# First up products cut by columns, GpSimd's sums behind the last norm, and the final residual in two bulk transfers

## The chip, the cores and the metric

The kernel runs on one core of a Trainium2 chip. The metric is the device time of one execution in microseconds (us), and the runs of a kernel are summed up by their median. The engines of the core work side by side, each through its own list of instructions in order, and wait for each other by semaphores: TensorE (PE; its weight loads are listed as PEld), VectorE (DVE), ScalarE (ACT), GpSimd (POOL), and SyncE (SP), which here issues nearly all transfers.

## The reference

One layer of a diffusion backbone on 128 context tokens and 512 latent tokens (640 in all), width 1024, in fp32. A mixer (pooling and neighbourhood attention, merged and projected) comes first, then the channel part, in which nearly all of the change lies:

```
def _conv_ffn(h, w_up, conv_w, conv_b, w_down):
    u = h @ w_up
    up = jnp.pad(u, ((0, 0), (1, 1), (0, 0)))
    u = up[:, :-2] * conv_w[0] + up[:, 1:-1] * conv_w[1] + up[:, 2:] * conv_w[2] + conv_b
    a, g = jnp.split(u, 2, axis=-1)
    return (jax.nn.silu(a) * g) @ w_down
...
    x = x + ga * _merge(pool, na, gp, gn, w_pool_proj, w_na_proj, w_o)
    h = _modulated_norm(x, norm_ffn_g, sf, cf)
    x = x + gf * _conv_ffn(h, w_up, ffn_conv_w, ffn_conv_b, w_down)
```

w_up is 1024 x 5632 (halves a and g of 2816 columns), w_down 2816 x 1024. The outputs are the two new x and the context's keys and values.

## The kernel before, in words

**Arithmetic.** A product of fp32 matrices is made of three matmuls: both factors are split into a high part (ScalarE rounds it, names ending in h or hi) and a low part (VectorE subtracts the high one from the original, names ending in l or lo; `split_to`, L132), and high x high, high x low and low x high are added up.

**Tokens.** There are five token tiles of 128; tile 0 is the context. The channel part works on two halves of the columns of the transposed h: the first half has HB = 322 columns (tiles 0 and 1 and the first 64 columns of tile 2, with margins for the convolution), the second half 320. `b1h`/`b1l` hold the first half of all eight blocks of 128 features, `b12h`/`b12l` and `b2h`/`b2l` the second half of features 0 to 511 and 512 to 1023.

**The end of the mixer.** The output product (L736 to L738) runs tile by tile; `residual` adds x, the norm of the tile is taken (L743 to L747, result `xn`), and `second_h` (L753) transposes the tile on TensorE (L759), scales and shifts it (L764, L767) and splits it into b1, b12 and b2. Its call for tile 4 stands after the first up products.

**The up product.** Its 22 groups f of 128 columns of a and of g are computed as follows. Group 0 goes plainly: `plain` (L899) multiplies 16 weight blocks with the first half of the columns, 48 matmuls, and later with the second half. From group 1 on, seven products take the place of eight, after Strassen's scheme: `up_a(f)` makes the two that need only original weights (A11 B11, A12 B21), while GpSimd makes four sums of weight blocks (`ws`, L859 to L862) from the raw loads; `up_w(f)` splits these sums and a22; `products_b` makes the other five with sums of h (`th`, `tl`; VectorE, L791 to L794 and L799). The last of the five, with A22, may start when VectorE has read the accumulator that it adds to (L888). `conv` makes the convolution for a and g: one step on ScalarE (L923), two on VectorE (L924, L925); then SiLU and the product (L941: GpSimd, for the last group VectorE), and the split into `ahi`/`alo`, for the last group into `th`/`tl`.

**The down product.** Every second f, `down_group` multiplies two groups with their rows of w_down (weights `dhi`/`dlo`, raw loads `raw<-in_wdn`), in ten pieces of a token tile and 512 columns, and VectorE adds each to `acc` (L978). The last four groups are done in `down_last` (L980): the first four pieces are begun early in accumulators of their own, up to their last group; each finished piece is added to acc (L1001), multiplied by the gate gf (`gfb`, L1002), and the residual x is added (L1003), which was stored in DRAM (`xscr`) and comes back piece by piece through `xr` (L999, three buffers). The last piece is cut in two of 256 columns.

**What sets the order.** The code is written in program order, and a scheduler sets the order of each engine from its own timeline; `keep_in_program_order` and `issue_after` pin single instructions. A pool with n buffers makes a writer wait until the reader of n earlier is done: `raw` has three, `ws` one. SP issues loads in its order, so one that waits for its buffer holds up those behind it.

## Time and profile before

| | us |
|---|---|
| median of three runs | 909.35 |
| lowest, highest | 908.69, 910.04 |
| the profiled execution | 908.53 |
| its span (first to last event in the trace) | 906.7 |
| TensorE busy in the span | 869.7 |
| VectorE busy | 669.9 |
| ScalarE busy | 394.6 |
| GpSimd busy | 232.9 |

Starts are counted from the start of the span. A row of a timeline gives start, duration, engine, line and operation, what it writes and reads, and in brackets how long its engine stood idle before and what ended that wait. Matmuls are pipelined: the time from start to start is what one costs, not its duration. The granted clock (PEclk) is that of TensorE, 1.00 for 2.4 GHz and 0.50 for 1.2 GHz.

### The profile page before, as it was taken

What the parts mean: (1) busy time and instruction counts of PE and PEld (TensorE: products, weight loads), DVE (VectorE), ACT (ScalarE), POOL (GpSimd) and SP (SyncE); (2) the same over time, 40 slices, a digit from 0 to 9 for tenths busy, and PEclk for the clock granted to TensorE, in tenths of its full rate; (3) what the DMA queues carried; (4) which work ended last, traced back from release to release, by engine and by line L of the source; (5) the groups of instructions that cost most, each with busy time, mean ns of one, the idle gap of its engine ahead of it and who ended that gap; (6) DMA issues with size and microseconds to landing.
All of it is one profiled execution on the core that took longest, in us unless ns stands there. A gap on an engine that the chain in (4) does not pass through costs nothing.

```text
span 906.7 us, 13346 instructions
## 1 busy us (share of the span) xinstructions
PE 869.7 (96%) x5234; PEld 781.0 (86%) x5234; DVE 669.9 (74%) x1000; ACT 394.6 (44%) x710; POOL 232.9 (26%) x179
## 2 busy tenths in 40 slices
...
DMA packets 33023, 112.20 MB, mean 124 GB/s; under 512 B 3856, under 2 KB 4528, under 8 KB 32704
## 3 DMA queue, kind: packets, MB, share of 16 engines
...
q14 instruction: 22, 0.18, 0.1%
...
## 4 chain that ended last, share of the span: by engine, by line
PE 77%; DVE 9%; DMA 7%; ACT 3%; issue 2%; POOL 1%; SPq 0%; DVEq 0%; ACTq 0%; POOLq 0%
PE acc L837 23%; PE acc L219 21%; PE sm L964 4%; PE sm L966 4%; PE sm L965 4%; PE acc L203 3%; PE acc L205 3%; PE acc L204 3%; DVE wlo L134 2%; ACT whi L133 2%; DMA raw<-in_wo 2%; DMA na<-in_xl 2%; DVE cv L924 1%; DMA raw<-in_wdn 1%; PE sm L541 1%
## 5 line engine op out<-in xcount | busy, mean ns | idle before, releaser
L133 ACT CAST whi<-raw 128x1024 fp32r<-128x1024 f32 (+1 forms) x86 | 81.2, 945 | 193.6 <-PE acc L837 77.0
L134 DVE TENSOR_TENSOR wlo<-raw,whi 128x1024 fp32r<-128x1024 f32 (+1 forms) x86 | 102.7, 1195 | 39.7 <-ACT whi L133 39.1
L837 PE MATMUL acc<-th,whi 128*128 128x322 f32 (+1 forms) x336 | 103.8, 313 | 4.2 <-ACT whi L133 2.2
L837 PE MATMUL acc<-tl,whi 128*128 128x322 f32 (+1 forms) x336 | 104.5, 311 | 0.0
L837 PE MATMUL acc<-th,wlo 128*128 128x322 f32 (+1 forms) x336 | 104.0, 311 | 0.0
L219 PE MATMUL acc<-hhi,whi 128*128 128x320 f32 x320 | 92.3, 322 | 0.4 <-ACT t L440 0.4
L219 PE MATMUL acc<-hlo,whi 128*128 128x320 f32 x320 | 90.1, 315 | 0.0
L219 PE MATMUL acc<-hhi,wlo 128*128 128x320 f32 x320 | 89.3, 315 | 0.0
L859 POOL TENSOR_TENSOR ws<-raw 128x512 f32<-128x512 f32 x21 | 30.7, 1462 | 176.5 <-DVE wlo L134 105.1
L965 PE MATMUL sm<-dlo,ahi 128*128 128x512 f32 (+1 forms) x188 | 74.0, 393 | 0.0
L964 PE MATMUL sm<-dhi,ahi 128*128 128x512 f32 (+1 forms) x188 | 71.4, 395 | 2.2 <-ACT dhi L133 1.7
L966 PE MATMUL sm<-dhi,alo 128*128 128x512 f32 (+1 forms) x188 | 71.4, 394 | 0.0
L837 PEld LDWEIGHTS acc<-th,whi 128*128 128x128 f32 x336 | 63.1, 189 | 8.0 <-ACT whi L133 4.4
L837 PEld LDWEIGHTS acc<-tl,whi 128*128 128x128 f32 x336 | 63.4, 189 | 1.4
L837 PEld LDWEIGHTS acc<-th,wlo 128*128 128x128 f32 x336 | 63.3, 189 | 1.2
L133 ACT CAST whi<-ws 128x1024 fp32r<-128x1024 f32 x42 | 43.1, 1047 | 42.6 <-PE acc L837 40.6
L219 PEld LDWEIGHTS acc<-hhi,whi 128*128 128x128 f32 x320 | 58.9, 193 | 2.8 <-issue 1.5
L837 PE MATMUL acc<-b1l,whi 128*128 128x322 f32 x184 | 57.6, 315 | 3.8 <-DVE b1l L134 3.8
L978 DVE TENSOR_TENSOR acc<-sm,acc 128x512 f32<-128x512 f32 x80 | 53.1, 682 | 9.2 <-PE sm L966 9.2
L219 PEld LDWEIGHTS acc<-hlo,whi 128*128 128x128 f32 x320 | 58.8, 192 | 0.8 <-issue 0.7
L219 PEld LDWEIGHTS acc<-hhi,wlo 128*128 128x128 f32 x320 | 58.2, 191 | 0.7 <-issue 0.5
L837 PE MATMUL acc<-b1h,whi 128*128 128x322 f32 x184 | 57.2, 314 | 0.9 <-ACT b1h L133 0.9
...
## 6 DMA issues: line engine op xcount, KB each, us to landing
...
```

Of the source, the lines that this page charges most:

```text
L133: nc.scalar.copy(hi, raw)
L134: nc.vector.tensor_tensor(out=lo, in0=raw, in1=hi.bitcast(F32), op=SUB)
L203: nc.tensor.matmul(ps[t], lhsT=xh, rhs=wh, start=(kt == 0), stop=False)
L204: nc.tensor.matmul(ps[t], lhsT=xh, rhs=wl, start=False, stop=False)
L205: nc.tensor.matmul(ps[t], lhsT=xl, rhs=wh, start=False, stop=(kt == KT - 1))
L219: nc.tensor.matmul(o[:, :n], lhsT=w[:, k], rhs=cut(x, k, c, n), start=st and a, stop=sp and b)
L837: upped[0] = nc.tensor.matmul(ps[:, cs], lhsT=a[:, c], rhs=b[:, k, cs], start=start and first, stop=last, skip_group_check=skip and not st ...
L859: nc.gpsimd.tensor_tensor(out=s[:, 1], in0=a21, in1=a22, op=ADD)
L964: nc.tensor.matmul(ps, lhsT=xh, rhs=hi[:, sl], start=first and j == js[0], stop=False)
L965: nc.tensor.matmul(ps, lhsT=xh, rhs=lo[:, sl], start=False, stop=False)
L966: nc.tensor.matmul(ps, lhsT=xl, rhs=hi[:, sl], start=False, stop=last and j == js[-1])
L978: nc.vector.tensor_tensor(out=o, in0=ps, in1=o, op=ADD)
```

## The change

Four edits. (1) `pool_mix`, the pooling mixer, is issued behind the last matmul of the gate products (`issue_after`). (2) `plain` makes its products in two cuts of the columns, 0 to 258 for both a and g, then 258 to 322; the ends of the first cut are the columns of tiles 0 and 1. (3) Of the four sums of group 1 on GpSimd, the third is written second, and the first and third wait for the norm of tile 4; the a22 split of group 1 stays in program order. (4) In `down_last` the stored x comes back in two transfers of 128 x 2560 elements into b1l and b1h, which nobody reads by then. For pieces 4 to 10, GpSimd multiplies acc by the gate and adds x ahead of the product, piece 4 behind the split of the last group; VectorE then multiplies the product by the gate into `tmp` and adds it.

```diff
@@ -131,7 +131,7 @@
 
     def split_to(raw, hi, lo):
         nc.scalar.copy(hi, raw)
-        nc.vector.tensor_tensor(out=lo, in0=raw, in1=hi.bitcast(F32), op=SUB)
+        return nc.vector.tensor_tensor(out=lo, in0=raw, in1=hi.bitcast(F32), op=SUB)
 
     def load_w(src, own=None):
         r = load_raw(src)
@@ -207,6 +207,8 @@
     def halves(w, kk):
         return tuple(x[:, kk * 512:(kk + 1) * 512] for x in w)
 
+    mt_last = [None]
+
     def mt_steps(outs, whi, wlo, xhi, xlo, nk, ncol, cut=lambda x, k, c, n: x[:, k, c:c + n]):
 
 
@@ -216,7 +218,8 @@
             st, sp = k == 0, k == nk - 1
             for w, x, a, b in ((wh, xhi, True, False), (wh, xlo, False, False), (wl, xhi, False, True)):
                 for o, (c, n) in zip(outs, ncol):
-                    nc.tensor.matmul(o[:, :n], lhsT=w[:, k], rhs=cut(x, k, c, n), start=st and a, stop=sp and b)
+                    i = nc.tensor.matmul(o[:, :n], lhsT=w[:, k], rhs=cut(x, k, c, n), start=st and a, stop=sp and b)
+                    mt_last[0] = i.ins
             yield
 
     def run(steps):
@@ -637,10 +640,12 @@
             split_to(pw, pwh, pwl)
         split_to(na[:, g, :], nhi[:, g, :], nlo[:, g, :])
         if pend:
-            pool_mix(*pend)
+            with tc.issue_after(mt_last[0]):
+                pool_mix(*pend)
         pend = (g, *d)
     t2s[4] = gate_na(4)
-    pool_mix(*pend)
+    with tc.issue_after(mt_last[0]):
+        pool_mix(*pend)
     eg.close()
     en.close()
     ex = ExitStack()
@@ -727,6 +732,8 @@
     for t in range(5):
         residual(acc[t], t, 0, sq0)
 
+    normed = []
+
     def out_product(t, mid):
         ps = ps_acc()
         for kt in range(KT):
@@ -744,7 +751,7 @@
         nc.scalar.activation(std, std, AF.Sqrt, bias=eps, scale=1.0 / D)
         nc.vector.reciprocal(std, std)
         xn = fp.tile([P, D], F32, name="xn2", bufs=2)
-        nc.scalar.activation(xn, x1[:, t, :], AF.Copy, scale=std)
+        normed.append(nc.scalar.activation(xn, x1[:, t, :], AF.Copy, scale=std).ins)
         return xn
 
 
@@ -856,9 +863,15 @@
         nc.scalar.copy(p1, pa[:, :HB])
         nc.vector.tensor_tensor(out=us["a"][f % 2][:, 1:1 + HB], in0=pb[:, :HB], in1=p1, op=ADD)
         s = fw.tile([P, 4, 512], F32, name="ws", bufs=1)
-        nc.gpsimd.tensor_tensor(out=s[:, 1], in0=a21, in1=a22, op=ADD)
+        first = nc.gpsimd.tensor_tensor(out=s[:, 1], in0=a21, in1=a22, op=ADD).ins
+        third = nc.gpsimd.tensor_tensor(out=s[:, 2], in0=a11, in1=a21, op=SUB).ins
+        if f == 1:
+
+            for i in (first, third):
+                tc.add_manual_dep(i, normed[-1].name,
+                                  mybir.DependencyInfo(mybir.DependencyClass.Sync, mybir.DependencyReason.DATA),
+                                  reason="behind the last norm")
         nc.gpsimd.tensor_tensor(out=s[:, 0], in0=s[:, 1], in1=a11, op=SUB)
-        nc.gpsimd.tensor_tensor(out=s[:, 2], in0=a11, in1=a21, op=SUB)
         nc.gpsimd.tensor_tensor(out=s[:, 3], in0=a12, in1=s[:, 0], op=SUB)
         ups[f] = pa, s, a22
 
@@ -870,7 +883,9 @@
                             (wp, s[:, 2:4].rearrange("p a b -> p (a b)"), 1024), (fw, a22, 512)):
             e = "" if tp_ is wp else "2" if n == 1024 else "3"
             hi, lo = [tp_.tile([P, n], F32R, tag=x + e, name=x + e, bufs=2 if tp_ is wp else 1) for x in ("whi", "wlo")]
-            split_to(src, hi, lo)
+            i = split_to(src, hi, lo)
+            if f == 1 and n == 512:
+                tc.keep_in_program_order(i)
             w += halves_of((hi, lo)) if n == 1024 else [(hi, lo)]
         ups[f] = pa, w
 
@@ -896,17 +911,20 @@
     split_to(rg, hi, lo)
     w0 = [halves_of(w0a), halves_of((hi, lo))]
 
-    def plain(x1_, x2_, n, c0):
-        for (wa, wb), u in zip(w0, (us["a"][0], us["g"][0])):
-            ps = ps_acc()
-            product(ps, wa, x1_, slice(0, n), start=True, more=True)
-            product(ps, wb, x2_, slice(0, n), skip=False)
-            nc.scalar.copy(u[:, c0:c0 + n], ps[:, :n])
-
-    plain(B11, B21, HB, 1)
+    def plain(x1_, x2_, cuts, c0):
+        ps = [ps_acc(), ps_acc()]
+        for a, b in zip(cuts, cuts[1:]):
+            for (wa, wb), p in zip(w0, ps):
+                product(p, wa, x1_, slice(a, b), start=True, more=True)
+                product(p, wb, x2_, slice(a, b), skip=False)
+        for u, p in zip((us["a"][0], us["g"][0]), ps):
+            nc.scalar.copy(u[:, c0:c0 + cuts[-1]], p[:, :cuts[-1]])
+
+
+    plain(B11, B21, (0, HCOL[1][1], HB), 1)
     second_h(4, xns[4])
     up_a(1)
-    plain(B12, B22, H2C, 1 + HB)
+    plain(B12, B22, (0, H2C), 1 + HB)
     sums(*J[2])
     for j in ((0, 192), (192, HB)):
         split_sums(*j)
@@ -925,6 +943,8 @@
         nc.vector.scalar_tensor_tensor(out=a, in0=u[:, 2:2 + AC], scalar=w[2], in1=a, op0=MULT, op1=ADD)
         return a
 
+    split_last = [None]
+
     def up_b(f):
         ua, ug = us["a"][f % 2], us["g"][0]
         if f:
@@ -939,7 +959,7 @@
             lo = fr.tile([P, AC], F32R, name="alo", bufs=3)
         nc.scalar.activation(a, a, AF.Silu)
         (nc.vector if f == NF - 1 else nc.gpsimd).tensor_tensor(out=a, in0=a, in1=b, op=MULT)
-        split_to(a, hi, lo)
+        split_last[0] = split_to(a, hi, lo).ins
         return hi, lo
 
     NG = NF // GRP - 1
@@ -982,25 +1002,45 @@
         pieces = [(t, c, 512) for t in range(5) for c in range(0, D, 512)]
         pieces[-1:] = [(4, 512, CUT), (4, 512 + CUT, CUT)]
         n = 2 * GRP
+
+        res = [x.rearrange("p a b -> p (a b)").bitcast(F32)[:, :5 * 512] for x in (b1h, b1l)]
+        for i, x in enumerate(res):
+            nc.sync.dma_start(x, xscr.rearrange("p t d -> p (t d)")[:, i * 2560:(i + 1) * 2560])
+
+        def place(i):
+            t, c, w = pieces[i]
+            k, e = divmod(t * D + c, 2560)
+            return acc[:, t, c:c + w], gfb[:, 1 if t == 0 else 0, c:c + w], res[k][:, e:e + w]
+
         early = {}
         for i in range(4):
             t, c, w = pieces[i]
             early[i] = ps_acc()
             down_piece(early[i], t, slice(c, c + w), range(n - 1), xs, ws, True, False)
+
+        for i in range(4, len(pieces)):
+            o, gate, x = place(i)
+            k = nc.gpsimd.tensor_tensor(out=o, in0=o, in1=gate, op=MULT).ins
+            if i == 4:
+                tc.add_manual_dep(k, split_last[0].name,
+                                  mybir.DependencyInfo(mybir.DependencyClass.Sync, mybir.DependencyReason.DATA),
+                                  reason="behind the last tile's chain")
+            nc.gpsimd.tensor_tensor(out=o, in0=o, in1=x, op=ADD)
         for i, (t, c, w) in enumerate(pieces):
             sl = slice(c, c + w)
+            o, gate, x = place(i)
             if i in early:
                 ps = early[i]
                 down_piece(ps, t, sl, range(n - 1, n), xs, ws, False, True)
+                nc.vector.tensor_tensor(out=o, in0=ps, in1=o, op=ADD)
+                nc.vector.tensor_tensor(out=o, in0=o, in1=gate, op=MULT)
+                nc.vector.tensor_tensor(out=o, in0=o, in1=x, op=ADD)
             else:
                 ps = (ps_acc if i % 2 else ps_small)()[:, :w]
                 down_piece(ps, t, sl, range(n), xs, ws, True, True)
-            xr = fr.tile([P, 512], F32, tag="xr", name="xr", bufs=3)[:, :w]
-            nc.sync.dma_start(xr, xscr[:, t, sl])
-            o = acc[:, t, sl]
-            nc.vector.tensor_tensor(out=o, in0=ps, in1=o, op=ADD)
-            nc.vector.tensor_tensor(out=o, in0=o, in1=gfb[:, 1 if t == 0 else 0, sl], op=MULT)
-            (nc.gpsimd if i < 7 else nc.vector).tensor_tensor(out=o, in0=o, in1=xr, op=ADD)
+                tmp = fr.tile([P, 512], F32, tag="xr", name="xr", bufs=3)[:, :w]
+                nc.vector.tensor_tensor(out=tmp, in0=ps, in1=gate, op=MULT)
+                nc.vector.tensor_tensor(out=o, in0=o, in1=tmp, op=ADD)
             dst = A["yc"] if t == 0 else A["yl"][(t - 1) * P:t * P, :]
             nc.sync.dma_start(dst[:, sl], o)
```

What this does to the lists of instructions, in the program's words; the lines of the changed kernel are its own (L844 is L837 of before, L766 L759, L745 L738, L866, L867, L874 and L875 are L859, L861, L860 and L862, L903 L888, L905 L890, L942 and L943 L924 and L925, L961 L941).

TensorE behind the last output product (L738), where b1h and b1l are the first half of h and xn_4460 is tile 3, before:

```order
L738 MATMUL acc<-w1h,mlo 128x512
L759 MATMUL sm<-ident,xn_4460 128x128 x8
L837 MATMUL acc<-b1h,whi 128x322
L837 MATMUL acc<-b1h,whi_4547 128x322
L837 MATMUL acc<-b1h,whi 128x322 x2
L837 MATMUL acc<-b1l,whi 128x322
```

And after, with xn_4522 for tile 4:

```order
L745 MATMUL acc<-w1h,mlo 128x512
L844 MATMUL acc<-b1h,whi 128x258
L844 MATMUL acc<-b1l,whi 128x258
...
L766 MATMUL sm<-ident,xn_4460 128x128 x4
L844 MATMUL acc<-b1h,wlo 128x258
...
L844 MATMUL acc<-b1h,whi 128x64
...
L766 MATMUL sm<-ident,xn_4522 128x128 x8
L844 MATMUL acc<-b1h,whi 128x322
```

The products of 258 columns stand directly behind the output product and around the transposes of tile 3, those of 64 behind all of them, and then the transposes of tile 4 and `up_a(1)`, as before.

VectorE in the last group but one and the last, where ua_4538 and ug_4540 are the up results of group 20 and ua_4539 of group 21, and the two wlo of 1024 elements are the last weights of the down product, before:

```order
L134 TENSOR_TENSOR wlo_8317<-raw,whi_8316 128x512
L924 SCALAR_TENSOR_TENSOR cv<-ug_4540,vec,cv 128x642
L925 SCALAR_TENSOR_TENSOR cv<-ug_4540,vec,cv 128x642
L890 TENSOR_TENSOR ua_4539<-acc,u_8333 128x320
L888 TENSOR_TENSOR ug_4540<-acc,p_8347 128x320
L134 TENSOR_TENSOR wlo<-raw,whi 128x1024
```

And after:

```order
L134 TENSOR_TENSOR wlo_8365<-raw,whi_8364 128x512
L134 TENSOR_TENSOR wlo<-raw,whi 128x1024
L942 SCALAR_TENSOR_TENSOR cv<-ug_4540,vec,cv 128x642
L905 TENSOR_TENSOR ua_4539<-acc,u_8381 128x320
L134 TENSOR_TENSOR wlo<-raw,whi 128x1024
L943 SCALAR_TENSOR_TENSOR cv<-ug_4540,vec,cv 128x642
L942 SCALAR_TENSOR_TENSOR cv<-ua_4539,vec,cv 128x642
L903 TENSOR_TENSOR ug_4540<-acc,p_8395 128x320
```

Both splits of 1024 elements and the first step of ua's convolution moved ahead of L888 (now L903).

GpSimd from the last sums on, where ws are the weight sums, before:

```order
L941 TENSOR_TENSOR cv<-cv 128x642
L859 TENSOR_TENSOR ws<-raw 128x512
L861 TENSOR_TENSOR ws<-raw 128x512
L860 TENSOR_TENSOR ws<-ws,raw 128x512
L862 TENSOR_TENSOR ws<-raw,ws 128x512
L941 TENSOR_TENSOR cv<-cv 128x642 x2
L1003 TENSOR_TENSOR acc<-acc,xr 128x512 x7
```

And after:

```order
L1023 TENSOR_TENSOR acc<-acc,gfb 128x512 x4
L866 TENSOR_TENSOR ws<-raw 128x512
L867 TENSOR_TENSOR ws<-raw 128x512
L1023 TENSOR_TENSOR acc<-acc,gfb 128x256 x2
L874 TENSOR_TENSOR ws<-ws,raw 128x512
L875 TENSOR_TENSOR ws<-raw,ws 128x512
L961 TENSOR_TENSOR cv<-cv 128x642
L1028 TENSOR_TENSOR acc<-acc,b1l 128x512 x4
L1028 TENSOR_TENSOR acc<-acc,b1l 128x256 x2
L961 TENSOR_TENSOR cv<-cv 128x642
L1023 TENSOR_TENSOR acc<-acc,gfb 128x512
L1028 TENSOR_TENSOR acc<-acc,b1h 128x512
```

The seven additions of the residual at the end are gone, and fourteen operations for pieces 4 to 10 stand before, between and behind the last sums and the two gated products (L941, now L961). On SP, the two transfers stand between the second and the third of the last four wdn loads; on ScalarE, the second dhi now stands behind the two whi of ws instead of ahead of them, and the first of the last two whi<-raw ahead of the convolution's step of ug.

## Rows read from the trace of the kernel before

**Rows 1.** The page: busy time, share of the span and instructions of each engine.

```profile
PE 869.7 (96%) x5234; PEld 781.0 (86%) x5234; DVE 669.9 (74%) x1000; ACT 394.6 (44%) x710; POOL 232.9 (26%) x179
```

**Rows 2.** Table of stretches; the columns are in its first row.

```profile
core 0: us, PE busy (x) PEld busy (x) DVE busy (x) ACT busy (x) POOL busy (x), PEclk, DMA share, GB/s
...
456.00:458.00 2.00, 0.00 (x0) 0.00 (x0) 2.00 (x4) 0.00 (x0) 1.43 (x1) 0.50 0.76 250
...
460.00:462.00 2.00, 2.00 (x10) 2.00 (x10) 2.00 (x7) 1.85 (x4) 0.00 (x0) 0.60 0.54 219
462.00:464.00 2.00, 2.00 (x16) 2.00 (x15) 2.00 (x4) 1.77 (x2) 0.00 (x0) 1.00 0.00 0
...
468.00:470.00 2.00, 2.00 (x15) 2.00 (x15) 1.76 (x5) 1.16 (x3) 0.00 (x0) 1.00 0.00 0
```

**Rows 3.** Timeline of TensorE in the first up products.

```profile
458.73 0.64 PE L837 MATMUL acc<-b1l,whi 128*128 128x322 f32 x1 [3.83 <-DVE b1l L134]
...
466.95 1.03 PE L759 MATMUL sm<-ident,xn 128*128 128x128 f32 x8
467.74 0.39 PE L837 MATMUL acc<-b1l,whi 128*128 128x322 f32 x1
...
471.36 0.56 PE L837 MATMUL acc<-b12h,whi 128*128 128x320 f32 x2
```

**Rows 4.** Timeline of VectorE in the same stretch.

```profile
452.34 3.97 DVE L134 TENSOR_TENSOR wlo<-raw,whi 128x1024 fp32r<-128x1024 f32 x2
456.23 1.48 DVE L791 TENSOR_TENSOR hf<-hf 128x256 f32<-128x256 f32 x1
...
471.33 0.70 DVE L134 TENSOR_TENSOR b12l<-hf,b12h 128x520 fp32r<-128x520 f32 x1 [0.42 <-ACT b12h L133]
```

**Rows 5.** Timeline of GpSimd, first and last of group 1's four sums.

```profile
450.59 1.27 POOL L859 TENSOR_TENSOR ws<-raw 128x512 f32<-128x512 f32 x1
...
455.83 1.59 POOL L862 TENSOR_TENSOR ws<-raw,ws 128x512 f32<-128x512 f32 x1
```

**Rows 6.** Timeline of ScalarE, the norm of tile 4.

```profile
461.87 1.15 ACT L747 ACTIVATE xn<-x,std 128x1024 f32<-128x1024 f32 x1
```

**Rows 7.** Timeline of TensorE at the end of the program.

```profile
858.08 0.41 PE L837 MATMUL acc<-th,whi 128*128 128x322 f32 x1 [2.05 <-ACT whi L133]
...
870.29 0.42 PE L837 MATMUL acc<-th,whi 128*128 128x322 f32 x1 [1.31 <-DVE ug L888]
...
899.98 0.28 PE L966 MATMUL sm<-whi,tl 128*128 128x256 f32 x1
```

**Rows 8.** Timeline of ScalarE at the end.

```profile
855.09 1.05 ACT L133 CAST dhi<-raw 128x1024 fp32r<-128x1024 f32 x1 [1.24 <-DMA raw<-in_wdn]
...
866.67 0.93 ACT L923 ACTIVATE cv<-ug,vec 128x642 f32<-128x642 f32 x1
```

**Rows 9.** Timeline of VectorE at the end.

```profile
867.63 0.89 DVE L924 SCALAR_TENSOR_TENSOR cv<-ug,vec,cv 128x642 f32<-128x642 f32 x1 [1.41 <-ACT cv L923]
...
869.76 0.48 DVE L888 TENSOR_TENSOR ug<-acc,p 128x320 f32<-128x320 f32 x1
...
898.71 0.69 DVE L1003 TENSOR_TENSOR acc<-acc,xr 128x512 f32<-128x512 f32 x1 [1.81 <-DMA xr<-xscr]
...
903.38 0.43 DVE L1003 TENSOR_TENSOR acc<-acc,xr 128x256 f32<-128x256 f32 x1 [0.20 <-DMA xr<-xscr]
```

**Rows 10.** Groups of instructions, shapes apart, VectorE from 833 to 907: busy, mean ns.

```profile
L134 DVE TENSOR_TENSOR wlo<-ws,whi 128x1024 fp32r<-128x1024 f32 x4 | 4.8, 1219 | 1.0 <-ACT whi L133 1.0
```

**Rows 11.** Timeline of GpSimd at the end.

```profile
842.76 1.29 POOL L859 TENSOR_TENSOR ws<-raw 128x512 f32<-128x512 f32 x1 [9.20 <-DVE wlo L134]
...
869.59 1.57 POOL L941 TENSOR_TENSOR cv<-cv 128x642 f32<-128x642 f32 x1 [14.95 <-DVE cv L925]
```

**Rows 12.** Timelines of VectorE and GpSimd in the loop of groups.

```profile
484.07 1.90 DVE L925 SCALAR_TENSOR_TENSOR cv<-ua,vec,cv 128x642 f32<-128x642 f32 x1
...
483.42 1.87 POOL L861 TENSOR_TENSOR ws<-raw 128x512 f32<-128x512 f32 x1
```

## The prediction

> **What bounds the kernel now.** I began with the busy shares: TensorE is busy 96% of the span [rows 1], so the change can pay only where TensorE stands still or where the program ends behind it. Two stretches matter. In the first, between the output product and the first up products, the table of stretches shows TensorE without work from 456 to 458 at a granted clock of 0.50, then ten matmuls in 2 us at 0.60, then sixteen at 1.00 [rows 2]. Its own timeline names the wait: 3.83 us for the split of b1l [rows 3]. VectorE, which makes b1l, is full all the while (2.00 of 2 us in three of the stretches, 1.76 in that from 468) [rows 2]: **the stretch is VectorE's**, and TensorE only shows it. In the second, the end, TensorE waits 2.05 us at 858.08 and 1.31 at 870.29, and its last product starts at 899.98 and takes 0.28 [rows 7]. VectorE's last addition starts at 903.38 and takes 0.43 [rows 9]: 3.55 us lie behind the last product.
>
> The profiled execution took 908.53 us, 0.82 below the median of the runs, 909.35. The sum is made on the execution; 0.8 is added for the median. About 0.2%, or 1.8 us, is what a measurement of this kernel can tell from no change.
>
> **Pooled mixing behind gates.** The order of all engines up to the last output product is the same in both programs. Cost 0.
>
> **First up products by columns.** The 48 matmuls of 322 columns become 48 of 258, which need only the first two tiles, and 48 of 64. A narrow matmul can't go faster than its weights are exchanged: eight transposes of 128 columns start at 466.95 and the next matmul at 467.74, so 0.099 us each [rows 3]. So 48 x 0.10 = 4.8 us for the narrow ones; 24 matmuls of 322 columns take 467.74 to 471.36, 0.15 each [rows 3], so one of 258 is between the two, some 0.125: 6.0 + 4.8 against 48 x 0.15 = 7.2 before, 3.6 us more work for TensorE. It lies in the idle of 3.83 and the smaller gaps ahead of it. The Trainium skill, "TensorE: Matmul & The Clock Gate", gives in "Back-to-back issue gap" an issue floor of about 25 ns for up to 64 columns, and in "LDWEIGHTS (loading the stationary operand)" 107 ns for 128 columns of weights; by the first the narrow ones would be an estimated 1.2 us, by the second 5.1, and the trace's 99 ns sides with the second.
>
> What does TensorE meet next? Before, the transposes of the last tile come at 466.95, 24 products follow, and at 471.36 TensorE takes the last tile's b12h, a moment before VectorE starts the split that makes b12l, at 471.33 [rows 3, 4]. TensorE could now be at the transposes at about 462, since the norm that they need would come earlier too, and at b12h at 462 + (471.36 - 466.95) = 466.4. But VectorE owes the same list of work until that split. Off this list go the a22 split (0.70, as the 520-element split at 471.33 [rows 4]) and idle time: 0.24 in 468 to 470 [rows 2] and the 0.42 before 471.33 [rows 4], 0.7 together. So the split starts at about 470 and TensorE **waits 3 to 4 us there in place of the 3.83**, unless contention falls.
>
> It doesn't fall, it moves. GpSimd's four sums ran from 450.59 to 457.42 [rows 5]; now two of them wait for the last norm, which was ready at 461.87 + 1.15 [rows 6], now perhaps at 460.5. Queued behind the wait on GpSimd are only the other sums, wanted by the later second half. Beside them before, two splits of VectorE (1024 elements and the 512 of a22; the row carries the first's shape) took 3.97 against 1.22 + 0.70, and a subtraction of 256 elements 1.48 [rows 4, 10] against 0.43 (the 256-element addition of [rows 9]): 3.1 us. In the loop the exchange is harsher: VectorE's step takes 1.90 next to a sum of 1.87 [rows 12] against 0.89 [rows 9], 1.0 a sum, 4.0 for four. So the move costs VectorE between -3.1 (if they meet nothing that minds) and +0.9. The Trainium skill, "GPSIMD Engine Reference", "8. Key points", says that GpSimd shares its SBUF interfaces with VectorE and contends with operations that have two SBUF inputs; the trace agrees with that 1.90 against 0.89, and by this rule any sum moved beside a full VectorE is paid again.
>
> And the clock: before, the ten matmuls at 0.60 against sixteen show (16 - 10) x 0.15 = 0.9 us lost in 2 us [rows 2], some 1.2 for the whole slow piece, and a wait of 3 to 4 us may bring it back at a worse place. The stretch: -1.4 (a22 and idle) + 0.5 (harsher meeting) + 0.9 (clock, later than before): **0**, between -1.4 - 3.1 = -4.5 and, with nothing of the 1.4 recovered, 0.9 + 1.2 = +2.1.
>
> **The end: sums of f=21 and the 2.05 us.** GpSimd's idle of 9.20 before 842.76 [rows 11] takes the first four gate multiplications, 4 x 1.29 = 5.2 us, as far as the accumulated pieces are ready. The two of 256 columns stand between the sums, 2 x 0.65 = 1.3 by half of 1.29. The last sum frees the buffer of the next wdn load, queued on SP, so load and the first dhi come up to 1.3 later. Against it, ScalarE's second dhi, which at 855.09 waited 1.24 for its load [rows 8], now stands behind both whi that TensorE waits for, worth up to 1.05. Between -1.1 and +1.4: **0**, as they cancel.
>
> **The end: VectorE around L888.** Before, the order is ug's second conv step, L890, L888 at 869.76 [rows 9], at once followed by TensorE's last twelve A22 products. Now two splits of 1024 elements stand ahead of L888, and a conv step of ua. Step by step: the 1024 whi (1.05) takes ScalarE's place of the conv's start at 866.67 [rows 8] and ends at 867.7; first split until 868.85 (1.22 each [rows 10], 1.15 from start to start); conv step (0.89 [rows 9]) until 869.75; L890 until 870.15; second split 871.3; two conv steps 873.1; L888 there in place of 869.76. **+3.3.** The first split fills the 1.41 that VectorE waited before 867.63 [rows 9], which is in that count.
>
> Besides, GpSimd's idle of 14.95 before 869.59 [rows 11] now holds six additions, 4 x 1.29 + 2 x 0.65 = 6.5 us, right where VectorE does these steps. At 1.0 each for the wide ones [rows 9, 12] that is 0 (idle, or inputs in PSUM, take them) to +4; I take +1.1, nearer to nothing met, since VectorE idled 1.41 there and GpSimd may be half through by then. A stall of 1.31 becomes one of 5 to 6; whether the clock falls in it as at 456 is open, 0 to 1.2, taken 0.5. **+4.9 in all, from +3.0 to +7.** Products after it shift along; their th/tl shift as well.
>
> **The end: the residual.** Eleven small loads become two of 1.31 MB on SP ahead of the last two wdn loads. At the 250 GB/s of 456 to 458 [rows 2] they take 10.5 us. They can start when TensorE has read b1h and b1l for the last time, an estimated 4 us before 858.08 (a product of 24 matmuls ahead of that wait), so they land by about 865; the pieces that need them come after the last product of the up stage, beyond 872. They can hold up the third wdn load, but its whi now has its place at 866.7 in the order. The last piece now has only a multiplication and an addition behind its product, 0.43 each by the additions of that size [rows 9], in place of 3.55, and no wait of 1.81 for xr [rows 9]. **-2.7**; if TensorE's own waits in the pieces grow, -1.8.
>
> The sum on the execution: 0 + 0 + 0 + 4.9 - 2.7 = +2.2, so 910.7, and 911.5 for the median.
>
> **Rivals.** (1) *VectorE recovers in the first stretch:* the sums behind the norm meet operations that don't mind, -4.5 there; with L888 at +3.0 and -2.7 that is -4.2, so 904.3 on the execution, 905.1. For it: VectorE's 1.76 of 2 at 468 is its only slack, so contention decides, and part of its work there is single-input. Against it: 2.00 of 2 in the other stretches shown [rows 2]. (2) *Level:* the order cost alone, 3.3, nothing met on GpSimd, clock kept; -2.7 and a gain of 0.5 at the first stretch: +0.1, 909.4. (3) *Slower by contention:* GpSimd's additions each cost VectorE 1.0 around L888, and the late sums delay the wdn loads. From two met additions on it is clearly slower; with four, +3.3 + 4.0 + 0.5 + 1.4 - 2.7 = +6.5, so 915.8. (4) *The split by columns does nothing:* the narrow products wait for the same b1l, 0 there; it is inside the forecast.
>
> **How the numbers follow.** Forecast (L888 with some contention, 910.5 to 913): 0.37. Level (907.5 to 910.5): 0.25. Slower by contention (913 to 916): 0.18. Faster (below 907.5): 0.20, half of it above 905.5. The range leaves out a tenth on each side: 905.5 to 915.5. Slower by over 0.2% begins at 911.2; of the forecast's chance 0.30 lies above: slower 0.48, same 0.32, faster 0.20.
>
> **What would show it.** In the profile after: no wait of TensorE for b1l, but one of 3 to 4 us for b12h or b12l near 466 to 470, with VectorE full; wrong if that wait is under 1.5. A wait of 4 to 6 us for L888 (L903 by the new lines) near 870 to 875; wrong if below 2.5. GpSimd's sums at 460 to 468 and VectorE's operations beside them at 1.5 to 1.9. The last VectorE operation 0.9 us behind the last product. The prediction fails if VectorE's steps before L888 overlap TensorE's earlier work, so that L888 isn't late, or if the first stretch gives its 4 us.

## The result, and the profile after

The changed kernel takes 915.25 us (median of 11 runs, 909.09 to 921.54) against 909.35 (11 runs, 906.82 to 912.73). These two medians lie 5.9 apart; the ratio on record is 1.0053, 95% interval 1.003 to 1.0077, or 4.8 us slower (2.7 to 7.0), and that is the figure used here. The profiled execution took 909.09 us with a span of 907.3, and was the shortest of its runs; before it was 908.53 with 906.7.

The two executions can't be laid side by side from their start. Up to the last matmul of the output product both run the same instructions in the same order, and yet that matmul starts at 449.85 before and here at 444.38. (It is the last L738 of before, L745 here.) In TensorE's timeline of the changed kernel it is the first row here, and the products by columns follow it at once.

```profile
444.38 0.39 PE L745 MATMUL acc<-w1h,mlo 128*128 128x512 f32 x1
444.61 0.28 PE L844 MATMUL acc<-b1h,whi 128*128 128x258 f32 x1
...
456.21 0.40 PE L844 MATMUL acc<-b1h,whi 128*128 128x64 f32 x1
```

So from here on places are counted from the start of that matmul ("behind the output product"), and kernels are compared by these distances. From it to the end of the span the changed kernel needs 907.3 - 444.38 = 462.9 us, the kernel before 906.7 - 449.85 = 456.9: **6.1 more**. That the span itself is only 0.6 longer is the other 5.5, which lie ahead of anything the change moves.

Where the 6.1 lie, by the distances of the copies of u (one for each group f from 1 on), of TensorE's waits and of the last product. A + is a distance behind the output product, and where only a difference stands, it is that between the two kernels' distances at the same place:

| place | before | after | difference |
|---|---|---|---|
| TensorE takes b12h | +21.5 | +21.3 | -0.2 |
| groups 2 to 6 of the loop | | | +1.3 to +1.4 |
| groups 16 to 20 | | | +0.9 to +1.1 |
| group 21: wait for whi | 2.05 | 2.88 | +0.8 |
| group 21: copy of u | | | +3.8, of which +2.9 is new since group 20 |
| wait for L888 (L903 after) | 1.31 | 4.58 | +3.3 new |
| from there to the last product | 29.69 | 31.16 | +1.5 new |
| start of the last product to the end of the span | 6.72 | 4.12 | -2.6 |

The table of stretches in the first part (it answers to [rows 2]; its columns are in its first row):

```profile
core 0: us, PE busy (x) PEld busy (x) DVE busy (x) ACT busy (x) POOL busy (x), PEclk, DMA share, GB/s
...
456.00:458.00 2.00, 2.00 (x13) 2.00 (x13) 2.00 (x2) 0.31 (x1) 1.92 (x2) 0.54 0.00 0
458.00:460.00 2.00, 2.00 (x11) 2.00 (x10) 1.97 (x3) 0.53 (x1) 0.80 (x1) 0.60 0.16 23
...
462.00:464.00 2.00, 0.77 (x6) 0.51 (x4) 2.00 (x5) 1.22 (x3) 0.00 (x0) 1.00 0.00 0
464.00:466.00 2.00, 0.35 (x2) 0.30 (x2) 1.63 (x4) 1.72 (x5) 0.00 (x0) 1.00 0.02 4
466.00:468.00 2.00, 1.83 (x8) 1.62 (x7) 1.97 (x5) 2.00 (x4) 0.00 (x0) 0.60 0.00 0
468.00:470.00 2.00, 2.00 (x10) 2.00 (x9) 2.00 (x4) 1.08 (x2) 0.00 (x0) 0.54 0.00 0
```

The idle of 456 to 458 in [rows 2] is gone: TensorE is busy from 444 to 462. But it is idle for 2.88 us in 462 to 466, and the granted clock falls twice: behind that wait (0.60, 0.54), and at 456 to 460 **while TensorE is busy** at the end of its 64-column matmuls. VectorE is full wherever it isn't waiting, and pays for GpSimd's sums (timelines of VectorE and of GpSimd, answering to [rows 4, 5]):

```profile
453.01 1.01 DVE L134 TENSOR_TENSOR b12l<-hf,b12h 128x512 fp32r<-128x512 f32 x1 [0.77 <-ACT b12h L133]
453.95 2.02 DVE L134 TENSOR_TENSOR tl<-hf,th 128x768 fp32r<-128x768 f32 x1
455.90 1.76 DVE L799 TENSOR_TENSOR hf<-hf 128x512 f32<-128x512 f32 x1
457.58 1.77 DVE L134 TENSOR_TENSOR b2l<-hf,b2h 128x512 fp32r<-128x512 f32 x1
...
459.99 0.95 DVE L134 TENSOR_TENSOR tl<-hf,th 128x768 fp32r<-128x768 f32 x1
```

```profile
452.20 1.28 POOL L866 TENSOR_TENSOR ws<-raw 128x512 f32<-128x512 f32 x1 [7.04 <-ACT xn L754]
...
457.19 1.61 POOL L875 TENSOR_TENSOR ws<-raw,ws 128x512 f32<-128x512 f32 x1
```

The same split of 768 elements takes 2.02 beside a sum and 0.95 without one, operations of 512 take 1.76 and 1.77 against 0.69: 0.3 + 1.1 + 1.1 + 1.1, some 3.5 us of VectorE in all.

At the end, the waits of TensorE that answer to [rows 7], ScalarE's casts to [rows 8], and VectorE's last operations to [rows 9]:

```profile
854.34 0.41 PE L844 MATMUL acc<-th,whi 128*128 128x322 f32 x1 [2.88 <-ACT whi L133]
...
855.61 0.63 PE L844 MATMUL acc<-b2h,whi 128*128 128x320 f32 x1 [0.42 <-ACT p L901]
...
872.02 0.39 PE L844 MATMUL acc<-th,whi 128*128 128x322 f32 x1 [4.58 <-DVE ug L903]
...
903.18 0.28 PE L986 MATMUL sm<-whi,tl 128*128 128x256 f32 x1
```

```profile
851.35 1.04 ACT L133 CAST dhi<-raw 128x1024 fp32r<-128x1024 f32 x1 [2.98 <-DMA raw<-in_wdn]
852.30 1.99 ACT L133 CAST whi<-ws 128x1024 fp32r<-128x1024 f32 x2
854.20 1.05 ACT L133 CAST dhi<-raw 128x1024 fp32r<-128x1024 f32 x1
```

```profile
866.31 1.23 DVE L134 TENSOR_TENSOR wlo<-raw,whi 128x1024 fp32r<-128x1024 f32 x1 [1.04 <-ACT whi L133]
...
871.38 0.49 DVE L903 TENSOR_TENSOR ug<-acc,p 128x320 f32<-128x320 f32 x1
...
903.95 0.43 DVE L1043 TENSOR_TENSOR acc<-acc,xr 128x256 f32<-128x256 f32 x1
```

and GpSimd there, for [rows 11]: its 9.20 us of idle are filled with gate products, and the last sum ends at 847.8, 403.4 behind the output product, where it ended at 849.0 before, 399.1 behind. The last row is the six additions of the residual.

```profile
831.28 1.30 POOL L1023 TENSOR_TENSOR acc<-acc,gfb 128x512 f32<-128x512 f32 x1 [2.31 <-DVE acc L998]
834.34 4.87 POOL L1023 TENSOR_TENSOR acc<-acc,gfb 128x512 f32<-128x512 f32 x3 [1.76 <-DVE acc L998]
...
846.01 1.76 POOL L875 TENSOR_TENSOR ws<-raw,ws 128x512 f32<-128x512 f32 x1
...
857.22 8.66 POOL L1028 TENSOR_TENSOR acc<-acc,b1l 128x512 f32<-128x512 f32 x6 [5.46 <-DMA b1l<-xscr]
```

### The profile page after: what moved, and what is told of

Same layout as the page of the kernel before. It is cut to its first block, busy times and chain, and to the rows that moved or that the text cites. A ratio compares the mean times of both kernels' runs of the same rounds, so it can differ in the third digit from the quotient of the medians.

```text
span 907.3 us, 13430 instructions
## 1 busy us (share of the span) xinstructions
PE 873.0 (96%) x5282; PEld 785.6 (87%) x5282; DVE 672.3 (74%) x1000; ACT 394.8 (44%) x710; POOL 242.7 (27%) x186
## 4 chain that ended last, share of the span: by engine, by line
PE 84%; DVE 7%; DMA 3%; ACT 2%; POOL 1%; issue 1%; SPq 0%; ACTq 0%; POOLq 0%; DVEq 0%
PE acc L844 24%; PE acc L221 22%; PE sm L984 5%; PE sm L986 5%; PE sm L985 5%; PE acc L203 4%; PE acc L205 4%; PE acc L204 4%; DVE wlo L134 2%; DMA na<-in_xl 1%; PE sm L544 1%; PE sm L528 1%; ACT whi L133 1%; PE sm L506 1%; PE acc L743 1%
## 5 line engine op out<-in xcount | busy, mean ns | idle before, releaser
L134 DVE TENSOR_TENSOR wlo<-raw,whi 128x1024 fp32r<-128x1024 f32 (+1 forms) x86 | 100.8, 1172 | 41.6 <-ACT whi L133 40.7
L844 PE MATMUL acc<-th,whi 128*128 128x322 f32 (+1 forms) x336 | 104.2, 314 | 8.1 <-DVE ug L903 4.6
L844 PE MATMUL acc<-tl,whi 128*128 128x322 f32 (+1 forms) x336 | 104.9, 312 | 0.0
L844 PE MATMUL acc<-th,wlo 128*128 128x322 f32 (+1 forms) x336 | 104.5, 312 | 0.0
L866 POOL TENSOR_TENSOR ws<-raw 128x512 f32<-128x512 f32 x21 | 31.0, 1477 | 168.7 <-DVE wlo L134 98.2
L844 PEld LDWEIGHTS acc<-th,whi 128*128 128x128 f32 x336 | 63.4, 190 | 11.5 <-issue 4.8
L844 PEld LDWEIGHTS acc<-tl,whi 128*128 128x128 f32 x336 | 63.8, 190 | 1.5
L844 PEld LDWEIGHTS acc<-th,wlo 128*128 128x128 f32 x336 | 63.8, 190 | 1.2
L844 PE MATMUL acc<-b1h,whi 128*128 128x322 f32 (+2 forms) x200 | 61.2, 308 | 0.0
L844 PE MATMUL acc<-b1l,whi 128*128 128x322 f32 (+2 forms) x200 | 61.0, 307 | 0.0
L134 DVE TENSOR_TENSOR wlo<-ws,whi 128x1024 fp32r<-128x1024 f32 x42 | 52.6, 1269 | 8.6 <-ACT whi L133 8.6
L844 PE MATMUL acc<-b1h,wlo 128*128 128x322 f32 (+2 forms) x200 | 58.5, 308 | 0.0
```

The lines of the kernel that those rows point to most:

```text
L134: return nc.vector.tensor_tensor(out=lo, in0=raw, in1=hi.bitcast(F32), op=SUB)
L844: upped[0] = nc.tensor.matmul(ps[:, cs], lhsT=a[:, c], rhs=b[:, k, cs], start=start and first, stop=last, skip_group_check=skip and not st ...
L866: first = nc.gpsimd.tensor_tensor(out=s[:, 1], in0=a21, in1=a22, op=ADD).ins
```

## The experiments

Totals are medians, and ratios go to the kernel before on the same chip (909.0 to 910.8 us). Where the table has one time alone, it is a single execution and says little, since these lie up to 10 us apart; the distances behind the output product, which come from one profiled execution of each kernel, are what is read there. "f=21 adds" is what the copy of u of group 21 is later than that of group 20, against before; "behind last product" runs from the start of the last product to the end of the span.

| run | ratio [95%] or one time, us | b12h taken at | groups 2 to 6 against before | f=21 adds | L888 wait | behind last product |
|---|---|---|---|---|---|---|
| before | | 21.5 | 0 | 0 | 1.31 | 6.72 |
| after | 1.0053 [1.003, 1.0077] | 21.3 | +1.4 | +2.9 | 4.58 | 4.12 |
| e_front | 1.0013 [0.9992, 1.0035] | 21.3 | +1.9 | +1.8 | 1.31 | 6.75 |
| e_cols | 909.85 | 21.8 | +0.3 | +0.5 | 1.31 | 6.43 |
| e_sums | 910.39 | 17.2 | -2.2 | +1.7 | 1.31 | 6.64 |
| e_sums5 | 0.9968 [0.9943, 0.9992] | 17.2 | -1.9 | -0.1 | 1.31 | 6.33 |
| e_front_tl | 1.0024 [1.0002, 1.0045] | 19.9 | -0.7 | +3.0 | 1.31 | 6.50 |
| e_front_130 | 1.0003 [0.9978, 1.0029] | 17.4 | +1.0 | +2.8 | 1.31 | 6.73 |
| e_fill | 909.24 | 21.3 | -0.2 | +2.9 | filled | 4.17 |
| e_tail | 1.0041 [1.0019, 1.0063] | 21.5 | -0.1 | +3.6 | 4.58 | 4.10 |
| e_tail_late | 1.0016 [0.9994, 1.0038] | 21.6 | +0.3 | +0.8 | 1.31 | 7.19 |
| e_after_l888 | 1.0020 [0.9999, 1.0042] | 21.3 | +1.4 | +2.7 | 2.53 | 4.18 |
| e_best7 | 1.0008 [0.9989, 1.0027] | 21.7 | +0.3 | +3.4 | 1.31 | 4.36 |
| e_mix | 0.9964 [0.9942, 0.9986] | 18.4 | -2.3 | +1.1 | 1.44 | 5.74 |

### The front half and the tail half apart: e_front, e_tail

**e_front** is the kernel before with the cut by columns and the gated sums (edits 2 and 3), **e_tail** the kernel before with `down_last` and its gate (edit 4).

```diff
 e_front:
-    plain(B11, B21, HB, 1)
+    plain(B11, B21, (0, HCOL[1][1], HB), 1)
 ...
+            for i in (first, third):
+                tc.add_manual_dep(i, normed[-1].name, ...)
 e_tail:
-            xr = fr.tile([P, 512], F32, tag="xr", name="xr", bufs=3)[:, :w]
-            nc.sync.dma_start(xr, xscr[:, t, sl])
+        res = [x.rearrange("p a b -> p (a b)").bitcast(F32)[:, :5 * 512] for x in (b1h, b1l)]
+        for i, x in enumerate(res):
+            nc.sync.dma_start(x, xscr.rearrange("p t d -> p (t d)")[:, i * 2560:(i + 1) * 2560])
+        for i in range(4, len(pieces)):
 ...
```

> The kernel before with only the first stretch changed (first up products in two cuts of columns, two sums of group 1 behind the last norm, a22 split kept in order). Length of the stretch from the last output product to the first product of the down stage: before 55.8 us, changed kernel 57.2. Theory (VectorE paces the stretch, the wait moves from b1l to b12h and takes the low clock with it): 57.2 again, wait for b12h 2.9, time +1.4 on before. Rival (the cut of columns gives its wait back, and all of the loss comes from the end): 52 to 54, time -2 to -4.

> The kernel before with only the end changed (residual in two transfers, GpSimd's gate products and additions where the scheduler puts them). From the first product of the down stage to the last product: before 394.4 us, changed kernel 401.6; from there to the end of the span 6.7 and 4.1. Theory (the end's order and GpSimd's early operations cost, the shorter close gains): 401.6 and 4.1, waits of 2.9 for whi and 4.6 for L888, each with a stretch at the low clock, time +4.7. Rival (the end alone gains, its loss in the changed kernel comes from the first stretch shifting it): 394 to 396 and 4.1, time -1 to -2.6.

Measured: e_front 1.2 us slower (-0.7 to 3.2), with a wait of 4.49 for b12h where 2.9 was expected, and e_tail 3.7 (1.7 to 5.7) where 4.7 was; together 4.9, beside the 4.8 of the whole change. Most of the loss is the tail's: its waits (3.13 for whi, 4.58 for L888) and its close (4.10) are near those of the changed kernel. Pooled mixing behind its gates (edit 1), which neither has, leaves no order changed up to the output product, and within these intervals it needs no share; it was not run alone.

### The clock: e_fill

The changed kernel with matmuls whose result nobody reads, 16 ahead of the wait for b12h and 20 ahead of the last A22 products, so that TensorE is busy through nearly all of both waits. They add work, and the scheduler, which sees them, also moved some conv steps and casts behind the first place.

```diff
+    def fill(ps, w, x, cs, n):
+        for _ in range(n):
+            tc.keep_in_program_order(nc.tensor.matmul(ps[:, cs], lhsT=w[0][:, :P], rhs=x[0][:, 0, cs], start=True, stop=True))
```

> The changed kernel with matmuls into an accumulator that is overwritten or never read where TensorE waits: 16 of 320 columns ahead of the last tile's b12h, 20 of 322 ahead of the last A22 products. They change no result and the engine's waits otherwise stay. Theory (each of these waits is followed by some 3 us at a granted clock of 0.50, worth 1.2 to 1.5 us): the clock behind both places is 1.00, the first stretch 57.2 becomes 55.8 or less, and the stretch from the first product of the last down stage to the last one 28.3 becomes 27.8. Rival (the low clock has nothing to do with the wait): it stays, and the stretches are the same or longer.

TensorE takes b12h at the same distance, 21.3, but the table of stretches shows 1.00 there and behind it:

```profile
469.00:471.00 2.00, 1.18 (x6) 0.69 (x6) 1.88 (x3) 2.00 (x6) 0.00 (x0) 1.00 0.01 4
471.00:473.00 2.00, 2.00 (x16) 2.00 (x15) 2.00 (x5) 1.58 (x3) 0.00 (x0) 1.00 0.00 0
```

16 matmuls in 2 us where the changed kernel has 10 at 0.54. TensorE's products behind the wait start some 1.4 us earlier than in the changed kernel from about 26 us behind the output product on, ahead of the moved steps, and the groups behind go from +1.4 to -0.2. So **the slow piece behind the wait accounts for the whole +1.4 of the front half**; the last stage (first matmul of the last products to the last) goes from 28.29 to 27.78, as before (27.80). The wait for b12h alone, with the clock kept, costs nothing against before, where b12h came no earlier.

### What takes the gain of the front: e_cols, e_sums, e_sums5

One edit of the front at a time: **e_cols** is edit 2, **e_sums** edit 3 (with the a22 split kept in order). **e_sums5** is the program of e_sums, timed over 12 runs.

```diff
 e_cols: the cut alone
-    plain(B11, B21, HB, 1)
+    plain(B11, B21, (0, HCOL[1][1], HB), 1)
 e_sums, e_sums5: the gated sums alone
+        if f == 1:
+            for i in (first, third):
+                tc.add_manual_dep(i, normed[-1].name, ...)
```

> The kernel before with the column cut of the first up products alone; GpSimd's sums of group 1 start when they did. Theory (VectorE sets when b12h of the last tile comes): the wait for b1l falls to about 1.5, one for b12h of 1 to 2 appears, b12h is taken 20.5 to 21.5 us after the last output product as in all kernels so far (21.3 to 21.6), the stretch is 55 to 56 us against 55.8. Rival (the cut alone gives its 3.8 back): b12h at 18 or less, 52 to 53 us.

> The kernel before with the sums of group 1 behind the last norm alone, the products not cut. Theory: b1l comes 3 us earlier, so TensorE waits 1 or less for it, and the time comes back as a wait of 2 to 4 for b12h at 21 us after the last output product; 55.5 to 57 us. Rival (sums beside the end of the chain cost VectorE nothing): b12h at 18.5 or less, 53 us.

> The kernel before with only the second tile's sums behind the last norm; the same edit as in the single look, now timed. The look showed b12h taken 17.2 us behind the last output product (21.5 before) and the groups of the loop 2.1 us earlier, of which the last group gave 1.7 back. Theory (the gain of this part is real and partly given back at the last group): 0.4 to 2.0 us faster than before. Rival (all given back): level within 0.4.

The gated sums alone are **faster than both kernels: 0.9968, 2.9 us (0.7 to 5.2)**, more than the 0.4 to 2.0 that was expected of e_sums5. TensorE takes b12h at 17.2 in place of 21.5. With the cut added to the same sums it takes b12h at 21.3: the cut costs four microseconds there. What does it is who meets whom. e_sums, timelines of VectorE and of GpSimd (L861 of its lines is the first sum, L859 of before and L866 after):

```profile
460.01 0.69 DVE L794 TENSOR_TENSOR hf<-hf 128x512 f32<-128x512 f32 x1
460.61 0.95 DVE L134 TENSOR_TENSOR tl<-hf,th 128x768 fp32r<-128x768 f32 x1
...
464.76 0.73 DVE L769 TENSOR_SCALAR hf<-sm,mA,mS 128x128 f32<-128x128 f32 x2
465.40 1.41 DVE L134 TENSOR_TENSOR tl<-hf,th 128x768 fp32r<-128x768 f32 x1
```

```profile
460.58 5.40 POOL L861 TENSOR_TENSOR ws<-raw 128x512 f32<-128x512 f32 x1 [8.45 <-ACT xn L749]
465.95 2.00 POOL L862 TENSOR_TENSOR ws<-raw 128x512 f32<-128x512 f32 x1
```

The first sum starts in a row of VectorE operations without a gap, and it is GpSimd that pays: 5.40 us in place of 1.28, the splits beside it at their 0.95. (5.41 in e_sums5, 5.40 in e_mix.) It ends 1.2 us behind the start of the TENSOR_SCALAR steps at 464.76, which read the transposes' accumulator, as if it had run only from there; in e_sums5 and e_mix too it ends 1.2 us behind VectorE's first such step or wait. In the changed kernel the first sum starts at 452.20, just as VectorE waits 0.77 us for b12h, and then VectorE pays, 2.02 for 0.95. That closes the account: VectorE's operations lose 3.5 us there and 0.5 in e_sums up to its split of b12l, it idles 1.2 us and 0.3, and that split starts at 21.3 and 17.5.

And the cut without the sums? e_cols, rows of its table of stretches, then the last tile's transposes on TensorE and the first step of VectorE that reads them:

```profile
462.00:464.00 2.00, 2.00 (x15) 2.00 (x15) 1.80 (x4) 2.00 (x6) 0.00 (x0) 0.69 0.00 0
464.00:466.00 2.00, 2.00 (x11) 2.00 (x11) 2.00 (x4) 0.79 (x2) 0.00 (x0) 0.50 0.00 0
```

```profile
464.46 1.97 PE L759 MATMUL sm<-ident,xn 128*128 128x128 f32 x8
```

```profile
468.37 0.40 DVE L767 TENSOR_SCALAR hf<-sm,mA,mS 128x128 f32<-128x128 f32 x1
```

The wait of 3.83 for b1l is gone (the longest now is 0.48), TensorE is busy without a break from 8.7 us behind the output product on, and from the last part of its 64-column matmuls the clock stands at 0.50 for 6.8 us, about 3.4 us of work lost. But that isn't what holds b12h at 21.8: the transposes end at 466.43 and VectorE comes to them at 468.37. It is full, with 0.6 us of idle in all from 2 us behind the output product to its split of b12l, as the expectation said; its waits of 1.5 and of 1 to 2 were 0.4 each. Whether the clock costs e_cols anything on top isn't shown.

### Gate and width: e_front_tl, e_front_130

**e_front_tl** is e_front with the sums gated later, behind the first written split of `split_sums` for tile 3. **e_front_130** is that with the cut at column 130.

```diff
 e_front_tl:
+            for i in (first, third):
+                tc.add_manual_dep(i, tl_split[0].name, ...)
 e_front_130:
-    plain(B11, B21, (0, HCOL[1][1], HB), 1)
+    plain(B11, B21, (0, HCOL[1][0], HB), 1)
```

> The kernel before, with the cut by columns and the gated sums, as in the run of both front parts; only the gate of the sums of group 1 is another: they wait for the first split of the third tile's sums (tl, 768 elements, on VectorE) in place of the last norm. Theory (who comes first): GpSimd took the port in the 0.77 us in which VectorE waited for a cast of b12h, 7.9 us behind the last output product, and then four operations of VectorE took 1.01, 2.02, 1.76 and 1.79 in place of 0.69, 0.95, 0.69 and 0.69, 3.6 us. With the gate behind that gap GpSimd's first sum starts inside a row of VectorE operations that follow one another without a gap, takes several us itself (5.40 in the run with the sums alone) and costs VectorE little: b12h is taken by TensorE 17.5 to 18.5 us behind the last output product (21.3 with both front parts) and group 2 onward stands 1 to 2 us earlier than in the kernel before, not 1.9 later. Rival (whoever meets pays): the four sums cost VectorE the same 3 to 4 us wherever they run beside it; b12h stays at 20.5 to 21.5. Second rival: the cut itself costs the time by its order, b12h at 20 or later though no operation of VectorE is lengthened.

> The same as the run with the cut and the sums gated on the split of the third tile's sums, but the 322 columns of the first up products are cut at 130 in place of 258, so that 48 matmuls of 130 columns and then 48 of 192 run where 48 of 258 and 48 of 64 ran; every engine's order is the same. In the run with 64 columns the granted clock was 0.50 from about 10 to 16.5 us behind the last output product while TensorE was busy throughout, and b12h was taken at 19.9. Theory (the stream of 64 columns brings the clock down): with 192 columns the clock stays at 1.00 from 8 to 17 us, TensorE reaches the transposes of the last tile some 3 us earlier, b12h is taken at 16.5 to 18.5 and the groups of the loop stand 1.5 to 3 us earlier than in the kernel before. Rival (the drop comes from something else in this stretch, as the operations beside it): the clock is at 0.50 again from about 10 to 16 and b12h at 19.5 to 20.5. Second rival: the 130 columns, which now come first, bring it down earlier, at 3 to 7 us, and b12h is at 20 or later.

e_front_tl missed its theory (17.5 to 18.5): 19.9, a tenth under its second rival. The sums are written behind that split too, not only gated by it. The split on which the gate hangs turned out to be the third in VectorE's order, so that the sums began at 14.7 and no operation of VectorE was lengthened before 16.6. Now TensorE was the late one: VectorE waited 0.77 and 0.44 us for its transposes, and the table of stretches says why.

```profile
458.00:460.00 2.00, 2.00 (x21) 2.00 (x20) 1.19 (x3) 2.00 (x5) 0.00 (x0) 1.00 0.00 0
460.00:462.00 2.00, 2.00 (x12) 2.00 (x12) 1.97 (x4) 1.19 (x3) 0.00 (x0) 0.51 0.00 0
462.00:464.00 2.00, 2.00 (x12) 2.00 (x11) 2.00 (x4) 0.84 (x1) 0.00 (x0) 0.50 0.00 0
```

With matmuls of 192 columns in the place of the 64 (e_front_130, about the same stretch, TensorE as busy):

```profile
460.00:462.00 2.00, 2.00 (x19) 2.00 (x18) 1.84 (x4) 1.86 (x4) 0.00 (x0) 1.00 0.00 0
462.00:464.00 2.00, 2.00 (x15) 2.00 (x14) 2.00 (x4) 0.89 (x4) 0.00 (x0) 1.00 0.00 0
```

The clock stays at 1.00 and b12h is taken at 17.4, as the theory said. It is one execution, and e_front, where the clock held beside the 64-column matmuls, is one against; but over all the kernels **the clock fell in or just behind the 64-column stream in five of six, and in none of the eight without it does a fall begin from 6 to 19 us behind the output product.** The rest of the theory fell. The groups stand 1.0 later, not 1.5 to 3 earlier: the sums, from 15.5 on, now lie beside the splits of the last tile, b12l takes 1.76 and b2l 1.77 in place of 0.70, TensorE waits 3.10 for b12l, and behind that wait the clock is at 0.50 again (timeline of VectorE):

```profile
467.95 1.76 DVE L134 TENSOR_TENSOR b12l<-hf,b12h 128x520 fp32r<-128x520 f32 x1
```

This run also limits what e_sums shows. Here too the first sum starts where VectorE has no gap, and yet it takes its usual 1.28 and VectorE pays, with 1.47 for 0.95 in the next split. What stands beside it is a pair of TENSOR_SCALAR steps:

```profile
464.07 0.72 DVE L769 TENSOR_SCALAR hf<-sm,mA,mS 128x128 f32<-128x128 f32 x2
464.86 1.47 DVE L134 TENSOR_TENSOR tl<-hf,th 128x768 fp32r<-128x768 f32 x1
```

```profile
464.23 1.28 POOL L874 TENSOR_TENSOR ws<-raw 128x512 f32<-128x512 f32 x1 [14.75 <-DVE tl L134]
```

So a full row of VectorE holds the sum off only while it is made of TENSOR_TENSOR steps; a wait, or a TENSOR_SCALAR step, lets it in.

Against what the expectation says, VectorE's order wasn't quite the same: the evacuations of the last tile's transposes moved in between the tl splits, so the 17.4 isn't the clock's alone.

### The end: e_after_l888, e_tail_late

**e_after_l888** is the changed kernel with the last two wdn splits and the conv steps of the last group put behind L888 on VectorE. **e_tail_late** is e_tail with all fourteen operations of GpSimd behind the last tl split.

```diff
 e_after_l888:
+            if j >= GRP:
+                tc.add_manual_dep(k.ins, ug_last[0].name, ..., reason='behind L888')
 e_tail_late:
-            if i == 4:
+            if True:
                 tc.add_manual_dep(k, split_last[0].name, ...)
```

> The changed kernel with the two splits of 1024 elements and ua's convolution steps of the last group put behind L888 again on VectorE. Theory (VectorE's order is the main cause of the wait of 4.6 before the last A22 products): that wait falls to 1 to 2, the low clock behind it is gone, 401.6 us from first to last down product become about 397, time -4.5 on the changed kernel, level with before. Rival (GpSimd's six additions beside VectorE are the cause): the wait stays at 3.5 or more, -1 at most.

> The kernel before with the end changed, and all of GpSimd's operations for pieces 4 to 10 behind the split of the last group, not piece 4 alone. VectorE's order around L888 is then the one of before. Theory (the loss at the end is where GpSimd's operations stand and what they do to the order): 394 to 395 us from the first down product to the last, 4.1 behind it, time -2.6. Rival (the two transfers of 1.31 MB hold up the wdn loads, or GpSimd's operations beside VectorE's in the last pieces cost as much there): 397 or more, time 0 or slower.

With VectorE's old order the wait for L888 falls from 4.58 to 2.53 (1 to 2 was expected), and the clock stays at 1.00 there, as the row of the table of stretches says:

```profile
872.00:880.00 8.00, 5.47 (x32) 4.82 (x32) 6.73 (x8) 5.25 (x7) 1.97 (x2) 1.00 0.00 0
```

The last stage takes 27.78; the total is 1.8 us over the kernel before, by the two ratios 3.0 under the changed one. So of the 3.27 that the wait grew, 2.05 are VectorE's order. The other 1.22 aren't GpSimd's additions. Ahead of L888 VectorE stands idle, for ScalarE's conv step of ug (timelines of VectorE and of ScalarE in e_after_l888):

```profile
873.23 0.89 DVE L945 SCALAR_TENSOR_TENSOR cv<-ug,vec,cv 128x642 f32<-128x642 f32 x1 [1.43 <-ACT cv L944]
```

```profile
871.34 1.04 ACT L133 CAST whi<-raw 128x1024 fp32r<-128x1024 f32 x1
```

The cast that the change puts ahead of that conv step is still there in this run: from the copy of ug to the conv step are 1.97 us, where it was 1.27. That is 0.7 of the 1.22; the rest isn't broken down. The additions do lengthen VectorE's steps beside them (in the changed kernel alo 1.81, conv 1.62 and 1.80 in place of 0.8 to 0.9), but they end at 865.88 there, VectorE then waits 1.04 for a cast (its row at 866.31), and from there to L888 its steps take what they take alone. The order, on VectorE and on ScalarE, is the whole of the 3.27 as far as the rows show.

In e_tail_late whi and L888 wait nearly as before (2.18 and 1.31), and the loss comes out at the close, as its rival said: GpSimd's timeline is full for 19.5 us beside the pieces, VectorE falls behind, and the span ends 7.19 behind the last product in place of 4.10.

```profile
875.97 8.64 POOL L1005 TENSOR_TENSOR acc<-acc,gfb 128x512 f32<-128x512 f32 x7 [7.78 <-DVE tl L134]
...
886.32 9.18 POOL L1010 TENSOR_TENSOR acc<-acc,b1l 128x512 f32<-128x512 f32 x6
```

The work on GpSimd isn't free at the close, and ahead of the last sums it delays a load (group 21, below); beside VectorE's steps ahead of L888 it lengthens them, but no wait of TensorE there comes of it.

### Two attempts at a better version: e_best7, e_mix

**e_best7** is the kernel before with four pieces prepared on GpSimd: gates behind the last sums, additions behind the last gated product of group 20, x in one transfer into b1l; the last additions of the earlier pieces go to VectorE. **e_mix** is e_sums with the casts of dhi behind the first whi, and x of the last four pieces in one transfer, behind the wdn loads, added by VectorE; GpSimd gets nothing new.

```diff
 e_best7:
+        for i in range(7, len(pieces)):
+            tc.add_manual_dep(nc.gpsimd.tensor_tensor(out=o, in0=o, in1=gate, op=MULT).ins, sum_last[0].name, NOSYNC, ...)
+            tc.add_manual_dep(nc.gpsimd.tensor_tensor(out=o, in0=o, in1=x, op=ADD).ins, mul_last[0].name, NOSYNC, ...)
 e_mix:
+            if g == NG - 1 and j < GRP:
+                tc.add_manual_dep(cast[0], mixed[0].name, ...)
+        k = nc.sync.dma_start(res, xscr.rearrange("p t d -> p (t d)")[:, x0:])
```

> The kernel before with the short close for the last four pieces only (7 to 10): one transfer of 128 x 1536 elements into b1l, GpSimd's four gate products behind the last weight sum, its four additions behind its last gated product; pieces 0 to 6 as before, their last addition on VectorE. Theory (the close gains 2.6 if GpSimd's work neither delays the sums, nor stands beside VectorE's steps before L888, nor beside the last pieces): from the first to the last down product 394.4 to 395.5, behind it 4.1, time -2 on before. Rival (GpSimd's four gate products beside the splits and the convolution cost VectorE 1.0 each): waits for whi or L888 grow by 1 to 3, time 0 to +1.

> The kernel before with three edits: the second tile's sums behind the last norm; the casts of the last two dhi behind the first cast of the last group's mixed weights on ScalarE, so that only one cast (whi2) is left when TensorE's products free its place; the residual of the last four pieces in one transfer into b1l's place behind the last wdn loads, added by VectorE, nothing new on GpSimd. Theory: -2.1 (sums), about -0.9 (a wait of 1.1 in place of 2.05 for whi near the end, clock kept), -1.9 (last VectorE operation 1.6 behind the last product in place of 3.55), and nothing lost at L888 (wait 1.31 as before): 904 to 906 where before has 909, 3.5 to 5 us faster. Rival: gains in the middle are given back by waits of the last group, and only the close stays: 907, 2 us faster.

e_best7 has its short close (4.36) and L888 at 1.31, and loses it at group 21, as its rival said: GpSimd's four gate products, from 847.50 to 853.66, stand beside VectorE's conv steps and its split of raw weights,

```profile
849.99 1.78 DVE L134 TENSOR_TENSOR wlo<-raw,whi 128x512 fp32r<-128x512 f32 x1
```

which takes 0.69 before. It ends at 851.77, and at 851.81 SP issues the second wdn load, 404.1 behind the output product, where it was 401.4; the transfer of x stands behind that load. ScalarE waits 3.14 for the second dhi, TensorE 4.03 for whi behind it. Level. e_mix is 3.3 us faster than before (1.3 to 5.3), no better than the sums alone, and under the 3.5 to 5 that were expected. Its wait for whi is 1.81, not 1.1, and followed by a slow piece; its close only 1.0 shorter, since GpSimd's additions of the earlier pieces still hold VectorE (1.07 for 0.69) in the pieces.

## Why the prediction was right and where it was wrong

The verdict (slower by over 0.2%, chance 0.48) and the range (905.5 to 915.5) held, the range by 0.25 us, which is luck. The size didn't: 915.25 lies 3.7 over the forecast and in the band of rival (3). Of that rival's two causes one came, the wdn loads that the late sums delay; the other, contention around L888, didn't. Step by step:

- **Pooled mixing, 0.** Nothing in the runs speaks against it: the two halves without it sum to the whole, within 2 us each.
- **First stretch, 0 taken, +1.3 to +1.4 measured,** inside -4.5 to +2.1. What VectorE would meet was read rightly: b12h at 21.3 against 21.5, in place of 3.83 a wait of 2.88 (named: 3 to 4; in e_front 4.49). The operations beside the sums took 1.76 to 2.02 (named: 1.5 to 1.9); the sums came earlier than named, from 7.8 to 14.4 behind the output product, where 460 to 468 is 10 to 18. The term that was mis-sized is the clock. 0.9 was taken for a slow piece "later than before"; e_fill shows that the one behind this wait is worth 1.4 to 1.6, which is all of the loss.
- **The rule that the sums are paid wherever they run (-3.1 to +0.9, taken +0.5) failed** as a rule on one edit: e_sums shows the gate alone near the gain end, 4.3 us earlier at b12h. The Trainium skill, "GPSIMD Engine Reference", "8. Key points", says that the two engines contend for shared SBUF interfaces; the rows agree, 2.02 against 0.95, but in e_sums the same pair of operations met and GpSimd's sum took the 5.40. With the cut the norm, and with it the sums, come in VectorE's gap of 0.77, and the prediction didn't look for gaps.
- **The narrow matmuls, 0.10 each.** They run at 0.111 apart (48 from 6.87 to 12.25 behind the output product, with the slow ones at the end). The Trainium skill, "TensorE: Matmul & The Clock Gate", "Back-to-back issue gap", has an issue floor of about 25 ns for one matmul taken by itself, by which 48 would take an estimated 1.2 us, and says that in a stream with weight loads both operations set the spacing; the trace shows 5.4 us. "The split by columns does nothing" (rival 4) was nearly the case, +0.3 in e_cols, since VectorE owes the same list, as the prediction said. What no term held is a fall of the clock in busy work. It cost nothing in the changed kernel; that the clock is lost only behind waits was the wrong picture all the same.
- **Sums of f=21, 0 taken, +2.9 measured,** outside -1.1 to +1.4. The mechanism was named (the gates push the sums, the sums hold the wdn load, the load holds the first dhi), its size was wrong. Three gates took 1.62 each, not 1.29, and waited for VectorE twice (2.31 and 1.76), so the load came 4.2 us later by the distance (403.4 against 399.2), not 1.3. The second dhi did stand behind both whi, which gave part of that back, but ahead of the copy of p, for which TensorE then waits another 0.42 (855.61). So there are 0.83 and 0.42 of waits and, behind them, a clock of 0.50 in 856 to 858 and 0.76 in 858 to 860, 1.5 us, for which nothing was taken; 0.2 isn't accounted for. The clock's part is not the tail's alone: e_front, e_sums, e_front_tl and e_front_130, which have no gates, lose it there too.
- **Around L888, +4.9 taken.** The wait grew by 3.27 to 4.58, in the named 4 to 6 us, and by what was foreseen, the order: 3.3 were taken for it, and the runs give all 3.27 to it. The contention with GpSimd's six additions, 1.1 taken, is the term that failed: they end 5.5 us before L903, VectorE waits 1.04 for a cast behind them, and no wait of TensorE comes of them. Behind the wait +1.5 more, where 0.5 stood for the clock (872 to 876 at 0.65 and 0.50; 0.5 of it in the last stage).
- **The close, -2.7 taken, -2.6 measured;** the last VectorE operation ends 0.92 behind the end of the last product (named: 0.9), where it was 3.55.
- **The sum:** +1.3 - 0.4 (drift in the loop) + 2.9 + 3.3 + 1.5 - 2.6 = +6.0 in this pair, against +2.2. The 3.8 between them are the first stretch's 1.3 and group 21's 2.9, less the drift. Around L888 the sum came out, 4.8 for 4.9, by luck: contention nothing for 1.1, clock 1.5 for 0.5. The granted clock has about 1.4 + 1.5 + 1.5 = 4.4 of the 6 us, and was taken at some 1.4. Over all runs the difference is 4.8 (2.7 to 7.0).

What group 21 adds in the other kernels follows two things, the wait for whi and whether the clock falls behind it. e_sums and e_sums5, one program, added 1.7 and -0.1 there. The waits are 2.42 and 1.97, and these are the stretches behind them, of e_sums and then of e_sums5:

```profile
860.00:862.00 2.00, 2.00 (x9) 2.00 (x9) 1.24 (x3) 0.14 (x1) 0.00 (x0) 0.50 0.39 154
```

```profile
860.00:862.00 2.00, 2.00 (x14) 2.00 (x15) 2.00 (x4) 0.85 (x2) 0.00 (x0) 1.00 0.71 229
```

0.45 is the wait and the other 1.3 or so the clock. In e_front_tl and e_front_130 (+3.0, +2.8) the waits are 1.6 and 1.5 longer than before, and the clock falls too. The length of the wait alone doesn't decide: behind 2.52 (e_cols) the clock held, behind 1.81 (e_mix) it fell.

What stays open: when the clock falls behind a wait of 1.8 to 2.5 us, and why in e_front_tl and e_front_130 the second wdn load takes 5.4 and 5.3 us from issue to landing (ScalarE waits 2.76 and 2.64 for it), against 3.8 before and in e_sums5, with the same queue ahead of it.
